# One query tile's rotation earlier, and other places for some of the work beside the matmuls, in a hybrid decoder layer's kernel

## The chip, the cores and the metric

The kernel runs on one core of one Trainium2 chip. The metric is the time of one execution on the device, in microseconds (us). Each kernel is run several times; the median is given with the lowest and the highest. One execution is recorded by the hardware profiler, and all rows come from that one.

## What is computed

A decoder layer in fp32: 512 tokens of 1024 channels. The normalised input is projected once (`h @ w_in`), and the pieces feed two branches, whose outputs are merged by sigmoid gates, projected by `w_out`, added to the input, and followed by a gated convolutional feed-forward layer.

```python
h = rmsnorm(x, norm1_w)
proj = h @ w_in
(mq, mk, mv, mo, mi, mf, nq, kc, vc, ks, vs, kw, vw, ng, gm, gn) = jnp.split(proj, split_pts, axis=-1)
...
hm = mlstm_chunkwise(...)                                  # 4 heads
hm = rmsnorm(hm, m_out_norm_w) * jax.nn.sigmoid(mo)
qn = apply_rope(rmsnorm(nq, q_norm_w), cos, sin)           # 8 heads of 64
...
on = gates[..., 0:1] * o_cmp + gates[..., 1:2] * o_slc + gates[..., 2:3] * o_win
y = jax.nn.sigmoid(gm + merge_gate_b[0]) * (hm @ w_up_m) \
    + jax.nn.sigmoid(gn + merge_gate_b[1]) * (on @ w_up_n)
x = x + y @ w_out
h2 = rmsnorm(x, norm2_w)
a, v = jnp.split(h2 @ ffn_w_up, 2, axis=-1)
a = jax.nn.gelu(causal_dwconv(a, ffn_conv_w, ffn_conv_b), approximate=False)
return x + (a * v) @ ffn_w_down
```

## The kernel before

**Matrix products.** The tokens are worked on in four tiles of 128 (`NT = 4`), the channels in eight groups of 128 (`KD = 8`). An fp32 product is three fp32r products on TensorE (PE): high by high, high by low and low by high, where high is a rounded copy and low is what the rounding left. The class `Weights` brings each weight chunk from memory into one of two raw buffers (`raw`, SP's queue) and `ensure` splits it, half a chunk at a time, into `whl`: four buffers, each with a high and a low half. The high half is a copy by ScalarE (ACT, L88). The low half comes in one of two ways: VectorE (DVE) subtracts (L94), or, for the halves in `on_dma`, ACT makes a negated copy (L91) and GpSimd (POOL) issues a DMA that adds the raw chunk to it (L92). PLAN's `pool...` entries say which: 2 puts a whole group into `on_dma`, and `poolWO` speaks of the first four halves of `w_out` alone.

**Order.** Nothing is scheduled by a tool: every engine works through its own list in the order in which the program wrote it. Two kinds of work are interleaved by hand. One is the layer's latency-bound part (rotation, attention, mLSTM). The other is a stream of projection matmuls, a generator wrapped in the class `Filler`: `fill(ns)` draws three matmuls at a time, each counted as 650 ns, until a balance `bal` is used up. The amounts stand in the table PLAN and are read with `FL(key, default)`. The stream's groups come as A, MV, GM, MO, MQK, GN (the projections of those names), and from the last mLSTM head on UN, the product of `on` with `w_up_n`, then UM, that of `hm` with `w_up_m` (`up_group`). A finished group of matmuls is evacuated by ACT or DVE a few draws later (`after`).

**Banks.** The accumulators lie in eight banks: two of `pa`, two tiles of two banks for `psS`, one `pt`, one `po`. Behind UM these pools are closed, and eight new banks `pf` hold the accumulators of `w_out`, named `wo00` to `wo31` (token tile, column half).

**The places that the change touches, in the order of the run.**

- The rotation of the queries. `rope_q(t)` rotates tile t (L680 to L688 on DVE, a part on POOL) and copies the result to be doubled (`qdup`, L235 on DVE for tiles 0 to 2 and L233 on ACT for tile 3, by PLAN's `p_dupq`). `q_transposes(t)` transposes it on PE into the banks `pt` and `po` (`pq`, L847), and `QS` is made from these by ACT (L849) and DVE (L850). Tile t + 1 is rotated behind the transposes of tile t. The A and MV groups' matmuls run in between (`aV`, `aVs`), and GM's after the last tile.
- The columns of the mLSTM's gates: `rows_b`, a generator stepped from within the attention loop, transposes rows into `uop` (L1083) in the bank `pt`, which the attention's transposes `ptp` use as well.
- The gates' sigmoids: `T["gm"]` (L1253) before the mLSTM's first head, `T["gn"]` (L1277) behind its last, each with ACT's table of functions loaded anew around it (L1255, L1273, L1278).
- The mLSTM's four heads. `mls_s` makes scores `mA` and `mB`, `mls_e` and `mls_x` the exponentials EA and EB, `mls_m` multiplies them (L1129, L1130 on DVE), `mls_b` multiplies by the values (`mo`, L1137 on PE), `mls_c` transposes, gates and splits the result (`hmH`, `hmL`). Between `mls_c(h)` and `mls_m` for head h + 1 the filler gets PLAN's `md{h}`, and before `mls_b` PLAN's `mb{h}`.
- The merge. `evac_un` (L742) and `evac_um` (L1298 to L1307) gate the products and add them. `wo` (L426 to L428) multiplies by `w_out`.
- The loads of x and of the second norm's weights are issued by POOL (L1333, L1335) between the tiles of the first four halves of `w_out`.

```python
    for h in range(4):
        ...
        fill(FL(f"mb{h}", 1000))
        hs, sc, ee = mls_b(h, ee[2], mid)
        ...
        fill(FL(f"mc{h}", 5000))
        mls_c(h, hs)
        if h < 3:
            fill(FL(f"md{h}", 2000))
            mls_m(sc, ee)
```

Of the kernel before, what the change touches and what calls it, by code (L numbers as in the profile page):

```python
# [9 lines left out]
AF = mybir.ActivationFunctionType  # L10
# [8 lines left out]
NT = S // P  # L19
# [78 lines left out]
def bcast(ap, n):  # L98
# [18 lines left out]
    "p_sc21": 0, "p_sc30": 0, "p_sc31": 1, "poolA": 2, "poolC": 0, "poolGM": 2, "poolGN": 2, "poolMO": 2,  # L117
    "poolMQK": 2, "poolMV": 0, "poolUM": 0, "poolUN": 3, "poolWO": 0, "q2_eb": 1, "q2_ex0": 0, "q2_ex1": 0,
# [42 lines left out]
def body(ctx, tc, I, out, dbg=None):  # L161
# [53 lines left out]
    def pt(name):  # L215
        return ps.tile([P, 512], F32, name=name, tag="pt", bufs=1)
# [279 lines left out]
                yield 650  # L496
                tick()

    def up_group(ids, mH, mL, evac, nm, flag):
        for m in range(KD):  # L500
            acc = (psS if m % 2 else pa)(f"{nm}{m}")[:, 0:512]
            W.ensure(ids[m // 2])
            H, L = W.hl[ids[m // 2]]
            w = slice((m % 2) * P, (m % 2) * P + P)
            for k in range(4):
                if k == 2 and m % 2 == 0:
                    W.ensure(ids[m // 2] + 3)
                pe.matmul(acc, H[:, k, w], mH[:, k, :], start=(k == 0), stop=False)
                pe.matmul(acc, H[:, k, w], mL[:, k, :], start=False, stop=False)
                pe.matmul(acc, L[:, k, w], mH[:, k, :], start=False, stop=(k == 3))  # L510
                if k == 3:
                    after(2, lambda m=m, acc=acc: evac(m, acc))
                    if m == KD - 1:
                        after(2, lambda: done.add(flag))
                yield 650
                tick()
# [513 lines left out]
    def rows_b():  # L1030
        ir, fr, t1, t2 = T["rows"]

        act.activation(t1, fr, AF.Abs)
        act.activation(t1, t1, AF.Exp, scale=-1.0)
        dve.tensor_scalar(t2, fr, 0.0, None, op0=ALU.min)
        yield
        act.activation(t1, t1, AF.Ln, bias=1.0)
        yield
        dve.tensor_sub(fr, t2, t1)
        on = onesf[0:4, :]  # L1040
        for c in range(NT):
            q = slice(c * P, (c + 1) * P)
            dve.tensor_tensor_scan(t2[:, q], on, fr[:, q], 0.0, ALU.mult, ALU.add)
        yield
        dve.tensor_sub(ir, ir, t2)
        mc = sm([4, 4], "mc", 1)
        for c in range(NT):
            q = slice(c * P, (c + 1) * P)
            dve.tensor_tensor_scan(fr[:, q], on, ir[:, q], mc[:, c:c + 1] if c else 0.0, ALU.mult, ALU.max)
            if c + 1 < NT:  # L1050
                e = (c + 1) * P - 1
                dve.tensor_add(mc[:, c + 1:c + 2], t2[:, e:e + 1], fr[:, e:e + 1])
        yield

        dve.tensor_add(t1, t2, fr)
        R3 = s4("mrowC", F32R)
        nH, nL = R3[0:4, 0:512], R3[32:36, 0:512]
        pool.tensor_scalar(R3[0:32, 0:512].rearrange("p (a c) -> p a c", a=4),
                           onesf[0:32, :].rearrange("p (o c) -> p o c", o=1).to_broadcast([32, 4, P]), 0.0, None,
                           op0=ALU.mult)  # L1060
        dve.tensor_scalar(fr, fr, -1.0, None, op0=ALU.mult)
        dve.tensor_copy(nH, fr)
        dve.tensor_sub(nL, fr, nH)
        T["nHL"] = R3[0:36, 0:512]
        yield "R4"

        R4 = vst[:, 1024:1792]
        n = 0
        T["urow"] = []
        for k, (i, j) in enumerate(pairs):  # L1070
            if i == j:
                cur = ir[:, j * P:(j + 1) * P]
            else:
                new = R4[0:4, n * P:(n + 1) * P]
                n += 1
                dve.tensor_scalar(new, cur, t2[:, i * P - 1:i * P], None, op0=ALU.add)
                cur = new
            T["urow"].append(cur)

        yield  # L1080
        p = pt("uop")
        for k in range(len(pairs)):
            pe.transpose(p[:, k * 4:k * 4 + 4], T["urow"][k], ident[0:4, 0:4])  # L1083
        for t in range(NT):
            pe.transpose(p[:, 40 + t * 4:44 + t * 4], T["rows"][2][:, t * P:(t + 1) * P], ident[0:4, 0:4])
        dve.tensor_copy(uoc, p[:, 0:40])
        act.activation(emc, p[:, 40:56], AF.Exp, scale=-1.0)
# [119 lines left out]
        rope(qview(t), dup(qd), qrs[:, t * 8:t * 8 + 8], 3, t, 1, 8, f"q{t}")  # L1207
        return qd

    qd = rope_q(0)  # L1210
    fill(FL("z14", 3900))
    for t in range(NT):
        q_transposes(t, qd)
        if t + 1 < NT:
            qd = rope_q(t + 1)
        if t == 1:
            pc0 = cmp_scores(0)
        if t == 2:
            cmp_exp(0, pc0)
        fill(FL(f"z16_{t}", 2600))  # L1220
        if t == 2:
            cmp_scale(0, pc0)
        if t == 3:
            cmp_transposes(0, pc0)
# [21 lines left out]
    for z in range(2):  # L1246
        mz = T["mo"][:, 2 * z:2 * z + 2, :]
        act.activation(mz, mz, AF.Sigmoid)
        fill(FL("z25", 1300))
    for i in range(2):  # L1250
        for z in range(2):
            g = T["gm"][i][:, 2 * z:2 * z + 2, :]
            act.activation(g, g, AF.Sigmoid)  # L1253
            fill(FL("z26", 1300))
    act.preload_act_table_set(LNEXP)  # L1255
    T["hmH"] = v4(page("hmH", F32R))
    sc = mls_s(0)
# [4 lines left out]
    for h in range(4):  # L1262
        if h < 3:
            mid = (lambda: mls_s(h + 1), lambda n: mls_e(h + 1, n), mls_x)
        else:
            mid = (lambda: None, lambda n: None, lambda n: None)
        fill(FL(f"mb{h}", 1000))
        hs, sc, ee = mls_b(h, ee[2], mid)
        if h == 3:
            fill.until(done, "GN")  # L1270
            fill = Filler(up_group(F_UN, T["onH"], T["onL"], evac_un, "un", "UN"), flush)
            W.ensure(F_UN[3])
            act.preload_act_table_set("sigmoid_and_others")  # L1273
            for i in range(2):
                for z in range(2):
                    g = T["gn"][i][:, 2 * z:2 * z + 2, :]
                    act.activation(g, g, AF.Sigmoid)  # L1277
            act.preload_act_table_set(LNEXP)  # L1278
        fill(FL(f"mc{h}", 5000))
        mls_c(h, hs)  # L1280
        if h < 3:
            fill(FL(f"md{h}", 2000))
            mls_m(sc, ee)
# [22 lines left out]
    def y_low(m):  # L1306
        dve.tensor_sub(act4(yL, m), T["gm"][m // 4][:, m % 4, :], act4(yH, m))  # L1307

    fill = Filler(up_group(F_UM, T["hmH"], T["hmL"], evac_um, "um", "UM"), flush)
    fill(1e9)  # L1310
    ps_cm.close()

# [336 lines left out]
```

## Time and profile before

| | |
|---|---|
| median of 3 runs | 793.24 us (791.92 to 793.84) |
| the profiled execution, its own time | 793.33 us |
| its span in the trace | 791.6 us |
| TensorE's mean granted clock | 0.998 of full speed |
| PE busy | 775.5 us, 98% of the span |
| DVE busy | 471.5 us, 60% |
| ACT busy | 371.1 us, 47% |
| POOL busy | 208.5 us, 26% |
| moved by DMA | 126.93 MB, 160 GB/s on average |

The span runs from the first to the last instruction of the core; the execution's own time has the start and the end around it, 1.7 us here. An engine's busy time is the time in which it worked on an instruction. PE's share is an upper bound of its use, since the ends of its pipelined matmuls are modelled. Times of rows are counted from the span's start: the query tiles' transposes lie at 97 to 117 us, the attention at 120 to 280, the mLSTM's heads at 290 to 349, UN and UM up to 393, `w_out` up to 425, and the feed-forward layer fills the rest.

### The profile page before, as it was taken

Reading aid. Unit: us, or ns where it says so; the run is one execution under the profiler, and the core shown is the slowest. Engines: PE = TensorE matmul, PEld = TensorE weight load, DVE = VectorE, ACT = ScalarE, POOL = GpSimd, SP = SyncE. Lnnn points to the kernel's source line nnn. Section 1 sums busy time; section 2 is a strip of 40 time slices with the busy share of each in tenths; the row PEclk is TensorE's granted clock in tenths of the full one; section 3 lists DMA queues with packets and bytes.
Section 4 is the critical chain, followed back from the end, with each engine's and each line's share of the span. In section 5 each row is a group of like instructions: output and inputs, shape, how many; then the busy total and the mean of one; then the engine's idle time right before and its main releaser. Section 6 shows DMA issues by size and latency. Waiting matters only on the chain.

```text
span 791.6 us, 10531 instructions
## 1 busy us (share of the span) xinstructions
PE 775.5 (98%) x4037; PEld 641.7 (81%) x4037; DVE 471.5 (60%) x827; ACT 371.1 (47%) x627; POOL 208.5 (26%) x217
## 2 busy tenths in 40 slices
PE   7999989999999999989999999999999999999997
PEld 5797878877888887878788998888888888888886
DVE  4576785676565654556755455455454554565865
ACT  6254536745565586464333243334334333455441
POOL 4420122120111113120000017854555443200700
PEclk9999999999999999999999999999999999999999
DMA  7884167655547476563263248665555434585472
GB/s 229 286 220 142 21 150 122 117 107 107 108 89 125 82 105 128 112 212 121 94 209 111 107 152 293 245 228 199 212 189 184 179 140 160 199 279 188 145 236 84
DMA packets 93314, 126.93 MB, mean 160 GB/s; under 512 B 6447, under 2 KB 72143, under 8 KB 91856
## 3 DMA queue, kind: packets, MB, share of 16 engines
q1 hardware_dynamic: 63054, 91.64, 34.8%
q0 software_dynamic: 30208, 34.61, 21.0%
q8 instruction: 32, 0.52, 0.3%
q14 instruction: 18, 0.15, 0.1%
q10 hardware_dynamic: 2, 0.00, 0.0%
HBM read 94.79 MB, written 15.73 MB: 140 GB/s over the span
## 4 chain that ended last, share of the span: by engine, by line
PE 84%; DVE 8%; ACT 4%; issue 1%; DMA 1%; SPq 0%; DVEq 0%; ACTq 0%
PE ff L1366 10%; PE ff L1365 10%; PE ff L1364 10%; PE P L427 4%; PE P L428 4%; PE P L426 4%; PE on L947 2%; PE ptp L936 2%; PE wo L426 2%; PE wo L428 2%; PE wo L427 2%; PE gm L488 1%; PE gm L490 1%; PE gm L489 1%; PE sp L906 1%
## 5 line engine op out<-in xcount | busy, mean ns | idle before, releaser
L94 DVE TENSOR_TENSOR whl<-raw,whl 128x1024 fp32r<-128x1024 f32 (+1 forms) x112 | 141.4, 1275 | 139.1 <-ACT whl L88 139.1
L88 ACT ACTIVATE whl<-raw 128x1024 fp32r<-128x1024 f32 (+2 forms) x144 | 144.8, 1012 | 121.2 <-PE ff L1366 57.1
L1364 PE MATMUL ff<-h2H,whl 128*128 128x512 f32 (+1 forms) x384 | 142.8, 372 | 0.0
L1365 PE MATMUL ff<-h2L,whl 128*128 128x512 f32 (+1 forms) x384 | 142.6, 371 | 0.0
L1366 PE MATMUL ff<-h2H,whl 128*128 128x512 f32 (+1 forms) x384 | 142.6, 371 | 0.0
L92 POOL DMA_DIRECT2D whl<-raw x30 | 43.6, 1454 | 183.7 <-ACT whl L91 175.6
L1365 PEld LDWEIGHTS ff<-h2L,whl 128*128 128x128 f32 x384 | 72.3, 188 | 12.6
L1364 PEld LDWEIGHTS ff<-h2H,whl 128*128 128x128 f32 x384 | 72.3, 188 | 12.5
L1366 PEld LDWEIGHTS ff<-h2H,whl 128*128 128x128 f32 x384 | 72.3, 188 | 12.4
L921 ACT ACTIVATE P<-sp,nmx 128x128 f32<-128x128 f32 (+3 forms) x64 | 33.1, 524 | 36.7 <-DVE nmx L912 36.5
L1416 ACT ACTIVATE ct<-ct 128x512 f32<-128x512 f32 x22 | 13.9, 634 | 54.1 <-DVE ct L1414 54.1
L912 DVE TENSOR_REDUCE nmx<-sp 128x2 f32<-128x256 f32 (+3 forms) x32 | 26.2, 818 | 17.9 <-PE sp L909 17.8
L426 PE MATMUL P<-whl,g 128*128 128x512 f32 x88 | 34.2, 389 | 0.0
L427 PE MATMUL P<-whl,g 128*128 128x512 f32 x88 | 34.2, 389 | 0.0
L428 PE MATMUL P<-whl,g 128*128 128x512 f32 x88 | 34.2, 389 | 0.0
L1414 DVE SCALAR_TENSOR_TENSOR ct<-ff,vcol,ct 128x511 f32<-128x511 f32 (+1 forms) x44 | 32.8, 744 | 2.2 <-ACT ct L1412 1.4
L91 ACT ACTIVATE whl<-raw 128x1024 fp32r<-128x1024 f32 x30 | 31.5, 1050 | 0.0
L1422 ACT ACTIVATE g<-ct 128x512 fp32r<-128x512 f32 x22 | 13.9, 634 | 37.0 <-DVE ct L1426 21.9
L235 DVE COPY P<-ptp 128x256 f32<-128x256 f32 (+1 forms) x32 | 17.7, 554 | 19.3 <-PE ptp L936 19.2
L1423 DVE TENSOR_TENSOR g<-ct,g 128x512 fp32r<-128x512 f32 x22 | 15.4, 699 | 22.0 <-ACT g L1422 22.0
L1355 POOL DMA_DIRECT2D x1d<-x x4 | 2.1, 536 | 95.1 <-DVE x L1354 95.1
L488 PE MATMUL gm<-hTH,whl 128*128 128x512 f32 x64 | 26.6, 416 | 0.0
(400 smaller groups left out, 1811.8 us busy)
## 6 DMA issues: line engine op xcount, KB each, us to landing
raw<-in_ffn_w_up_dram SPq DMA_DIRECT2D x22, 1024.0 KB, 5.1
raw<-in_w_in_dram SPq DMA_DIRECT2D x16, 1024.0 KB, 4.9
whl<-raw POOLq DMA_DIRECT2D x30, 512.0 KB, 5.7
st<-in_ffn_w_down_dram SPq DMA_DIRECT2D x11, 1024.0 KB, 7.0
td<-st POOLq DMA_DIRECT2D x11, 1024.0 KB, 4.1
raw<-td SPq DMA_DIRECT2D x22, 512.0 KB, 5.2
raw<-in_ffn_w_down_dram SPq DMA_DIRECT2D x11, 512.0 KB, 4.6
raw<-in_w_out_dram SPq DMA_DIRECT2D x4, 1024.0 KB, 4.9
```

The source lines that it names most:

```text
L88: nc.scalar.activation(h, src, AF.Copy)
L92: nc.gpsimd.dma_start(l, src, accum_op=ALU.add)
L94: (nc.gpsimd if n in self.on_pool else nc.vector).tensor_sub(l, src, h)
L426: pe.matmul(o, aH, bH, start=start, stop=False)
L427: pe.matmul(o, aH, bL, start=False, stop=False)
L428: pe.matmul(o, aL, bH, start=False, stop=stop)
L488: pe.matmul(acc, H[:, k, :], hh, start=(k == 0), stop=False)
L921: act.activation(Pv[:, y], sv[:, y], AF.Exp, bias=nmx[:, y:y + 1], accum_out=den[:, y:y + 1])
L1364: pe.matmul(acc[:, a:b], H[:, k, :], hh, start=(k == 0), stop=False)
L1365: pe.matmul(acc[:, a:b], H[:, k, :], hl, start=False, stop=False)
L1366: pe.matmul(acc[:, a:b], L[:, k, :], hh, start=False, stop=(k == KD - 1))
L1414: dve.scalar_tensor_tensor(t[:, k:], a[:, :S - k], col("ffn_conv_w", (2 - k) * NF + m), t[:, k:], op0=ALU.mult, op1=ALU.add)
```

## The change

Six things move; no arithmetic is left out or added.

- `rope_q` runs one tile ahead: tiles 0 and 1 before the loop, tile t + 2 behind the transposes of tile t.
- `rows_b` draws three matmuls more ahead of `uop`, and takes their 650 ns off the balance again.
- The four sigmoids of `gm` go from ahead of the first head to behind `mls_c(3)`, one before every 1300 ns of filler, and the table load behind `gn`'s sigmoids goes behind them.
- `md2` becomes 0: the multiplications of the last head follow `mls_c(2)` at once, and the filler that stood between them comes after.
- `up_group` gets a list `wide` of the groups that go to `psS` banks: it was the odd ones; now it is 1, 3, 6, 7 for UN and 1, 6, 7 for UM.
- `poolWO` becomes 2: the low halves of `w_out`'s first four weight halves come from L91 and the DMA of L92.

```diff
-    "mc0": 4675, "mc1": 5000, "mc2": 5000, "mc3": 11500, "md0": 3950, "md1": 3625, "md2": 15275, "ms0": 6300,
+    "mc0": 4675, "mc1": 5000, "mc2": 5000, "mc3": 11500, "md0": 3950, "md1": 3625, "md2": 0, "ms0": 6300,
...
-    "poolMQK": 2, "poolMV": 0, "poolUM": 0, "poolUN": 3, "poolWO": 0, "q2_eb": 1, "q2_ex0": 0, "q2_ex1": 0,
+    "poolMQK": 2, "poolMV": 0, "poolUM": 0, "poolUN": 3, "poolWO": 2, "q2_eb": 1, "q2_ex0": 0, "q2_ex1": 0,
...
-    def up_group(ids, mH, mL, evac, nm, flag):
+    def up_group(ids, mH, mL, evac, nm, flag, wide):
         for m in range(KD):
-            acc = (psS if m % 2 else pa)(f"{nm}{m}")[:, 0:512]
+            acc = (psS if m in wide else pa)(f"{nm}{m}")[:, 0:512]
...
         yield
+        fill(650)
+        fill.bal -= 650
         p = pt("uop")
...
-    qd = rope_q(0)
+    qds = [rope_q(0), rope_q(1)]
     fill(FL("z14", 3900))
     for t in range(NT):
-        q_transposes(t, qd)
-        if t + 1 < NT:
-            qd = rope_q(t + 1)
+        q_transposes(t, qds[t])
+        if t + 2 < NT:
+            qds.append(rope_q(t + 2))
...
-    for i in range(2):
-        for z in range(2):
-            g = T["gm"][i][:, 2 * z:2 * z + 2, :]
-            act.activation(g, g, AF.Sigmoid)
-            fill(FL("z26", 1300))
     act.preload_act_table_set(LNEXP)
...
-            fill = Filler(up_group(F_UN, T["onH"], T["onL"], evac_un, "un", "UN"), flush)
+            fill = Filler(up_group(F_UN, T["onH"], T["onL"], evac_un, "un", "UN", (1, 3, 6, 7)), flush)
...
-            act.preload_act_table_set(LNEXP)
         fill(FL(f"mc{h}", 5000))
         mls_c(h, hs)
+        if h == 3:
+            for i in range(2):
+                for z in range(2):
+                    fill(1300)
+                    g = T["gm"][i][:, 2 * z:2 * z + 2, :]
+                    act.activation(g, g, AF.Sigmoid)
+            act.preload_act_table_set(LNEXP)
...
-    fill = Filler(up_group(F_UM, T["hmH"], T["hmL"], evac_um, "um", "UM"), flush)
+    fill = Filler(up_group(F_UM, T["hmH"], T["hmL"], evac_um, "um", "UM", (1, 6, 7)), flush)
```

How this moves instructions is shown at three places, where a queue's order decides. Rows are an engine's instructions in its own order: line, operation, out<-in, shape. Lines of the changed kernel are two or three higher there from `uop` on.

ACT from the QS of query tile 1 to that of tile 2, before:

```order
L849 ACTIVATE QS_859<-pq_1070 128x512
L849 ACTIVATE QS_859<-pq_1077 128x512
L233 ACTIVATE vst<-sc_1092 128x256
L88 ACTIVATE whl_1104<-raw_910 128x1024
L91 ACTIVATE whl_1104<-raw_910 128x1024
L849 ACTIVATE QS_860<-pq_1123 128x512
L849 ACTIVATE QS_860<-pq_1130 128x512
L233 ACTIVATE qdup_1137<-qdup_1137 128x8x64
```

and with the change:

```order
L849 ACTIVATE QS_859<-pq_1078 128x512
L849 ACTIVATE QS_859<-pq_1085 128x512
L233 ACTIVATE qdup_1092<-qdup_1092 128x8x64
L233 ACTIVATE vst<-sc_1100 128x256
L88 ACTIVATE whl_1112<-raw_910 128x1024
L91 ACTIVATE whl_1112<-raw_910 128x1024
L849 ACTIVATE QS_860<-pq_1131 128x512
L849 ACTIVATE QS_860<-pq_1138 128x512
```

The copy of the rotated tile 3 (`qdup`) stood behind the QS of tile 2 (`QS_860`); it now stands ahead of the copy of the scores (`vst`), of the weight half (`whl`, L88 and L91) and of that QS.

DVE from the end of head 2 to the multiplications of the last head (`EA`, `EB` with `mA`, `mB`), before:

```order
L1167 SCALAR_TENSOR_TENSOR hs_3257<-mhT_3327,vcol,mo 128x512
L1169 TENSOR_TENSOR hmL<-hs_3257,hmH 128x512
L94 TENSOR_TENSOR whl_3337<-raw_3182,whl_3337 128x1024
L1129 SCALAR_TENSOR_TENSOR EA_3263<-mA_3236,EA_3263 128x896
L1130 SCALAR_TENSOR_TENSOR EB_3264<-mB_3237,EB_3264 128x384
L1143 TENSOR_TENSOR mad<-mad,emc 128x4
```

and with the change:

```order
L1169 SCALAR_TENSOR_TENSOR hs_3253<-mhT_3323,vcol,mo 128x512
L1171 TENSOR_TENSOR hmL<-hs_3253,hmH 128x512
L1131 SCALAR_TENSOR_TENSOR EA_3259<-mA_3232,EA_3259 128x896
L1132 SCALAR_TENSOR_TENSOR EB_3260<-mB_3233,EB_3260 128x384
L94 TENSOR_TENSOR whl_3335<-raw_3178,whl_3335 128x1024
L1145 TENSOR_TENSOR mad<-mad,emc 128x4
```

The subtraction for a weight half (L94) stood ahead of the multiplications and now stands behind them.

POOL from the last heads' masks on (`EA_`, `EB_`) to the writes of the new x (`x1d`), before:

```order
L1124 AFFINE_SELECT EA_3263<-EA_3263 128x128 x2
L1124 AFFINE_SELECT EB_3264<-EB_3264 128x128 x2
L92 DMA whl_3297<-raw_3036 128x4x256
L1333 DMA x_0_3537<-in_x_dram 128x1024 x2
L1335 DMA nw_3540<-in_norm_w_dram 128x1024
L1333 DMA x_1_3538<-in_x_dram 128x1024 x2
L1355 DMA x1d<-x_0_3537 128x1024 x2
```

and with the change:

```order
L1126 AFFINE_SELECT EA_3259<-EA_3259 128x128 x2
L1126 AFFINE_SELECT EB_3260<-EB_3260 128x128 x2
L92 DMA whl_3293<-raw_3032 128x4x256
L92 DMA whl_3590<-raw_3511 128x1024
L92 DMA whl_3628<-raw_3511 128x1024
L92 DMA whl_3668<-raw_3588 128x1024
L92 DMA whl_3724<-raw_3588 128x1024
L1336 DMA x_0_3537<-in_x_dram 128x1024 x2
L1338 DMA nw_3540<-in_norm_w_dram 128x1024
L1336 DMA x_1_3538<-in_x_dram 128x1024 x2
L1358 DMA x1d<-x_0_3537 128x1024 x2
```

Four DMAs for the low halves of `w_out` (`whl_3590` to `whl_3724`) are new, and the loads of x and of the norm's weights (`nw`) stand behind them.

## Rows read from the trace of the kernel before

**Rows 1.** who PE waited for: us in total, times, longest us

```profile
PE mo L1137 <- DVE EA L1129: 2.1, 1, 2.1
...
PE pq L847 <- DVE qdup L235: 1.8, 3, 1.1
...
PE wo L426 <- DVE gm L1298: 1.0, 1, 1.0
...
PE gn L488 <- ACT gn L719: 0.6, 1, 0.6
PE pq L847 <- ACT qdup L233: 0.6, 1, 0.6
PE uop L1083 <- DVE P L235: 0.5, 1, 0.5
```

**Rows 2.** timeline of PE in a dense run: start us, us, engine, line, operation, out<-in

```profile
206.18 0.40 PE L489 MATMUL mo<-hTL,whl 128*128 128x512 f32 x1
206.41 0.39 PE L490 MATMUL mo<-hTH,whl 128*128 128x512 f32 x1
```

**Rows 3.** timeline of DVE at the rotation: [idle before <-releaser] at the end

```profile
93.05 0.69 DVE L680 TENSOR_TENSOR qraw<-qraw,rrs 128x512 f32<-128x512 f32 x1
...
96.18 0.52 DVE L235 COPY qdup<-qdup 128x512 f32<-128x512 f32 x1
96.61 1.21 DVE L94 TENSOR_TENSOR whl<-raw,whl 128x1024 fp32r<-128x1024 f32 x1
98.14 1.30 DVE L850 TENSOR_TENSOR QS<-pq,QS 64x512 fp32r<-64x512 f32 x2 [0.32 <-ACT QS L849]
...
116.36 0.69 DVE L235 COPY mv<-aV 128x512 f32<-128x512 f32 x1
```

**Rows 4.** timeline of ACT at the rotation

```profile
106.54 1.05 ACT L91 ACTIVATE whl<-raw 128x1024 fp32r<-128x1024 f32 x1
...
115.57 0.63 ACT L233 ACTIVATE qdup<-qdup 128x512 f32<-128x512 f32 x1 [3.99 <-DVE qdup L688]
```

**Rows 5.** timeline of PE at the transposes of the query tiles

```profile
96.84 1.07 PE L847 MATMUL pq<-ident,qdup 128*128 128x128 f32 x8 [0.32 <-DVE qdup L235]
...
116.25 1.09 PE L847 MATMUL pq<-ident,qdup 128*128 128x128 f32 x8 [0.57 <-ACT qdup L233]
```

**Rows 6.** DMA issues: KB each, median us from issue to landing

```profile
whl<-raw POOLq DMA_DIRECT2D x30, 512.0 KB, 5.7
...
x<-in_x_dram POOLq DMA_DIRECT2D x4, 512.0 KB, 9.4
```

**Rows 7.** timeline of ACT ahead of the mLSTM's first head

```profile
292.05 3.89 ACT L1253 ACTIVATE gm<-gm 128x1024 f32<-128x1024 f32 x4
```

**Rows 8.** timeline of ACT behind the last head

```profile
353.22 1.28 ACT L1273 ACT_TABLE_LOAD   x1
354.51 3.91 ACT L1277 ACTIVATE gn<-gn 128x1024 f32<-128x1024 f32 x4
...
365.80 1.07 ACT L88 ACTIVATE whl<-raw 128x1024 fp32r<-128x1024 f32 x1 [0.27 <-PE un L510]
```

**Rows 9.** timeline of PE, first matmul of um

```profile
371.04 0.39 PE L508 MATMUL um<-hmH,whl 128*128 128x512 f32 x1
```

**Rows 10.** timeline of DVE ahead of the last head's mo

```profile
342.44 1.23 DVE L94 TENSOR_TENSOR whl<-raw,whl 128x1024 fp32r<-128x1024 f32 x1 [0.25 <-ACT whl L88]
343.58 1.08 DVE L1129 SCALAR_TENSOR_TENSOR EA<-mA,EA 128x896 f32<-128x896 f32 x1
```

**Rows 11.** windows: us, busy per engine, granted clock (PEclk), DMA share, GB/s

```profile
344.00:348.00 4.00, 3.19 (x15) 3.22 (x16) 1.13 (x2) 0.17 (x1) 0.68 (x2) 0.61 1.06 257
392.00:394.00 2.00, 1.00 (x6) 0.53 (x4) 1.97 (x3) 0.00 (x0) 0.00 (x0) 1.00 0.00 0
```

**Rows 12.** timeline of ACT, high halves of w_out's first four weight halves

```profile
378.67 1.05 ACT L88 ACTIVATE whl<-raw 128x1024 fp32r<-128x1024 f32 x1
...
397.05 2.94 ACT L88 ACTIVATE whl<-raw 128x1024 fp32r<-128x1024 f32 x3
```

## The prediction

> **What bounds the kernel now.** Read the table of busy times first: TensorE (PE) is busy for 98% of the span, the next engine for 60%. Work of PE is neither added nor taken away, so what can be won is what PE waits. The view of who waited for whom gives that directly [rows 1]: mo for EA (2.1 us), pq for qdup (1.8 in three waits, and 0.6), wo for gm (1.0), gn for gn (0.6), uop for P (0.5). The parts of the change answer to these one by one.
>
> Two things on pricing such a wait. Idle time is counted from the listed end of the matmul before: a listed matmul lasts 0.39 us, but the next of a dense run starts 0.23 later [rows 2]. So each wait is, from start to start, about 0.16 longer than its entry. And behind the merge no wait of PE is long enough for an entry in rows 1, so I count what is won earlier as won at the end.
>
> **The change part by part**, on the clock of the profiled run.
>
> *Rotation one tile ahead.* DVE takes 3.6 us for one tile's rotation with its copy (93.05 to 96.6), 3.1 without the copy, 1.2 for the low part of a weight half and 1.3 for both QS of a tile [rows 3]. Before, each rotation began behind QS of the tile before it, and PE came for the tile too early. The change starts tile 1 before the loop. I walk DVE by these durations: tile 1 from 96.6 to 100.2, the half to 101.3, QS of tile 0 to 102.6; tile 2 to 106.2, QS of tile 1 to 107.5; tile 3 to 110.6. Tiles 1 and 2 are there before PE.
>
> But tile 3's copy is ACT's, and in ACT's queue (first pair of order fences) it now stands ahead of the scores' copy, both passes of a weight half and QS of tile 2, which used to be ahead of it. The second of those passes began at 106.54 and takes 1.05 like the first; tile 3's copy takes 0.63 [rows 4]. So ACT now stands until the rotation is through, near 110.6, and comes to QS of tile 2 at 110.6 + 0.6 + 2.1, near 113.3; DVE's part of it ends near 115.2. Tile 3's transposes write over tile 2's banks. They began at 116.25 [rows 5]; without the waits before them PE is there near 114.2, and waits some 0.5. Next GM's first matmul needs the bank that DVE's copy of mv frees. That copy ended at 117.05 [rows 3], and behind the late QS it ends near 116.85. What is won at the first three waits is lost at these two: **0.2 us**. Ends: 0, if ACT's queue is that much slower; 2.1, if none of it reaches PE (rows 1: 1.8 + 0.6, less the first tile's 0.3 [rows 5], which stays). Of these I take the walked value. The late weight half's accumulating DMA lands 5.7 after its issue [rows 6], near 119, and GM's second group begins 24 matmuls (5.4 us) after 116.9: nothing.
>
> *Columns' transposes.* Three mo matmuls (0.69 by rows 2) that stood behind the scores now run while uop waits for P's copy, and the filler's balance is put back, so none is added. The wait is 0.5 [rows 1], 0.66 from start to start: **0.65**, ends 0 and 0.69.
>
> *Gates' sigmoids.* Four sigmoids of gm (3.89 us from 292.05 [rows 7]) stand ahead of ACT's table load, head 0's exponentials and the copy of gn for which PE waits 0.6 [rows 1]. Without them that copy moves up by nearly 3 us (the exponentials then wait for DVE). The whole wait goes: **0.8**, ends 0 and 0.8.
>
> They come back behind the last head, with the table load after them. The weight half that ACT began at 365.80 [rows 8] then begins near 369.3, behind the last head's copy, another half, 3.9 us of sigmoids and 1.3 of load. DVE's low part of it (1.2) and the evacuation of un6 (0.7) queue behind it and end near 372.2. um's second group needs un6's bank 12 matmuls, or 2.7 us, after 371.04 [rows 9]: 373.8. I cost it at nothing; the cover is 1.5 us, and a microsecond beyond it is a microsecond lost. In rows 8 a load of 1.28 starts at 353.22 and the next ACT instruction at 354.51, at once. The Trainium skill (ScalarE: Activation LUTs, What ACT_TABLE_LOAD costs) adds a drain of about 1.38 us to the load; by that, un6's evacuation would end near 373.6 and the cover be 0.2, the sum the same. The trace does not agree; rival 3 gets a little of its chance from it.
>
> *Last head's multiplications.* Before, DVE was free at 342.2, waited 0.25 for ACT, made the low part of a half (342.44, 1.23) and only then EA (343.58, 1.08) [rows 10]; PE, out of filler, waited 2.1, or 2.2 from start to start. Now EA stands ahead of the half (second pair of fences): 342.2 to 343.2, and PE goes on near 343.3 instead of 344.8. **1.5** are won, a wait of 0.7 stays; ends 0 and 2.2.
>
> Behind this wait the granted clock is 0.61 from 344 to 348 us [rows 11], a mix of the two levels, 2.4 and 1.2 GHz: 4 x (1 - 0.61) = 1.56 us of full-speed work lost. From 392 to 394 PE stands idle for 1.0 us and the granted clock stays 1.00 [rows 11]. A wait of 0.7 is nearer to that one, so I take the clock's **1.5** as won; ends 0 and 1.6.
>
> *Banks of the merge, and w_out's low halves.* With um's groups on other banks, wo's first matmul takes a bank whose reader is long done; the groups that meet um6's and um7's banks come 9 and 15 matmuls later (2.0 and 3.4 us). The wait of 1.0 goes [rows 1]: **1.15**, ends 0 and 1.2. For each of four low halves ACT takes a second pass (1.05) and POOL an accumulating DMA (5.7 to its landing [rows 6]) in place of DVE's 1.2. The first of these halves begins on ACT at 378.67 [rows 12], so it lands near 386.5; wo needs it when um's 96 matmuls are through, 371.04 + 21.8 = 392.8. The fourth begins at 397.05 [rows 12], lands near 404.9 and is needed 72 matmuls later, at 409.1. Cover 6.3, falling to 4.2: nothing on the path. The loads of x and of the norm's weights are now behind these four DMAs in POOL's queue (third pair of fences). They go out from about 400 and take 9.4 [rows 6]; x is first added when w_out's first tile is whole, 96 + 24 matmuls or 27 us after 392.8. Nothing.
>
> *Sum:* 0.2 + 0.65 + 0.8 + 1.5 + 1.5 + 1.15 = 5.8. The profiled run took 793.33, 0.09 above the median shown (793.24): **787.5 us**.
>
> **The rivals.**
>
> 1. *The waits go whole.* ACT's queue at the rotation doesn't reach PE (2.1 instead of 0.2), and EA comes 0.7 earlier still. For it: both hang on places in queues that I walked by hand. Against: ACT's order holds QS. 5.8 + 1.9 + 0.7 = 8.4: 784.9.
>
> 2. *The clock falls all the same.* PE meets 0.7 of idle and then the same short multiplications. Against: the second stretch of rows 11. 1.5 less: 789.0.
>
> 3. *um waits for un6's bank.* The late sigmoids and their load use up the cover of 1.5 and as much again (1.4). For it: ACT's queue there holds five things whose starts I moved. 788.9.
>
> 4. *w_out's low halves come late*, the slower side. They go through POOL's queue one after another, and the fourth stalls PE once it lands over 5.7 + 4.2 = 9.9 us after its ACT passes; each microsecond more is one lost. The nearest slow row, the loads of x with 9.4 on the same queue [rows 6], just doesn't do it. At 20 us, 10.1 are lost: 787.5 + 10.1 = 797.6; to end above the time before by over 0.3% it takes 18. The Trainium skill (DMA: Bandwidth & Descriptors, SWDGE vs HWDGE vs iDMA) says that GpSimd writes such a DMA's descriptors into SBUF, from which DVE shuts it out in its 2-port mode; no run here shows which of DVE's merge work is in that mode. The 30 DMAs of this kind landed in a median of 5.7 with DVE at work beside them, so this adds little to the chance.
>
> 5. *Nothing comes through.* PE's waits go, and the same time turns up as new waits in the feed-forward part, where weights come in behind PE all the time: about 793.2.
>
> **How the numbers follow.** 0.3% (2.4 us) is about what a measurement of this kernel can tell from no change, so faster means under 790.9. Chances: the forecast 0.52, rival 1 0.12, rival 2 0.15, rival 3 0.08, rival 4 0.05, rival 5 0.08. Faster: the first four, 0.87; same: rival 5, 0.08; slower: rival 4, 0.05. The range leaves out rivals 4 and 5 (0.13): from rival 1's 784.9, rounded down to 784.8, to rivals 2 and 3 together, 787.5 + 1.5 + 1.4 = 790.4.
>
> **What would show it.** Right: no entry for gn, uop and wo in the view of waits, and one of about 0.6 for mo; a granted clock of 1.00 in the four microseconds behind it; between 107 and 116 us an ACT that stands for DVE's rotation, PE's waits there moved to tile 3's pq and to gm; the accumulating DMAs x34. Wrong: a wait of wo for whl or for a DMA, of um for gn, a half clock behind a wait of 0.7, or new entries behind 420 us.

## The result, and the profile after

| | before | the change |
|---|---|---|
| median, same runs | 793.36 us (791.92 to 793.84, 4 runs) | 786.93 us (786.64 to 787.16, 4 runs) |
| ratio | | 0.9923, 95% interval 0.9911 to 0.9936 |
| profiled execution, its own time | 793.33 us | 786.64 us |

The change is faster by 0.8%: 6.4 us between the medians, where 5.8 had been forecast. The page of the changed kernel, its span, the engines' busy times and DVE's and POOL's groups for the weights' low halves:

```profile
span 784.8 us, 10544 instructions
...
PE 773.2 (99%) x4037; PEld 640.5 (82%) x4037; DVE 466.5 (59%) x823; ACT 374.5 (48%) x631; POOL 211.3 (27%) x221
...
L94 DVE TENSOR_TENSOR whl<-raw,whl 128x1024 fp32r<-128x1024 f32 (+1 forms) x108 | 136.5, 1276 | 148.7 <-ACT whl L88 148.7
...
L92 POOL DMA_DIRECT2D whl<-raw x34 | 47.1, 1384 | 234.9 <-ACT whl L91 183.9
```

PE has the same 4037 matmuls. Four low halves have gone from DVE's subtraction to POOL's DMA (x34 instead of x30). Who PE waited for in the changed kernel (us in total, times, longest us), to be laid beside [rows 1]:

```profile
PE gm L488 <- DVE mv L235: 1.0, 1, 1.0
PE pq L847 <- DVE QS L850: 0.9, 1, 0.9
...
PE mo L1139 <- DVE EA L1131: 0.6, 1, 0.6
...
PE pq L847 <- DVE qdup L235: 0.2, 1, 0.2
```

The entries of wo, gn and uop are gone, mo waits 0.6 instead of 2.1, and pq for qdup has only the first tile's wait left. Two entries are new, both at the rotation.

**Where the time went.** The same matmul can be looked up in both traces. How much earlier PE starts it in the changed kernel, in us, read at both ends of each place (0.2 of it is there from the kernel's first matmul groups on, ahead of every change):

| place | PE earlier, ahead of it | behind it | won there | forecast |
|---|---|---|---|---|
| rotation (from pq of tile 0 to gm's first matmul) | 0.23 | 0.41 | 0.2 | 0.2 |
| uop, with the three matmuls moved ahead of it | 0.37 | 0.95 | 0.6 | 0.65 |
| gn before the first head | 0.96 | 2.03 | 1.1 | 0.8 |
| last head, the wait | 2.03 | 3.51 | 1.5 | 1.5 |
| last head, the clock | 3.51 | 5.16 | 1.65 | 1.5 |
| wo | 5.15 | 6.39 | 1.25 | 1.15 |
| the feed-forward part | 6.39 | 6.38 | 0 | 0 |

The two profiled executions differ by 6.7 (793.33 and 786.64); the 0.3 that the table leaves lie outside PE's matmuls. PE's rows before, at gm's first matmul and at the last head:

```profile
117.10 0.50 PE L488 MATMUL gm<-hTH,whl 128*128 128x512 f32 x1
344.81 2.47 PE L1137 MATMUL mo<-mv,EA 128*128 128x129 f32 x10 [2.06 <-DVE EA L1129]
348.68 0.47 PE L508 MATMUL un<-onH,whl 128*128 128x512 f32 x1
```

and of the changed kernel, for the last head:

```profile
341.30 1.35 PE L1139 MATMUL mo<-mv,EA 128*128 128x129 f32 x10 [0.57 <-DVE EA L1131]
343.52 0.48 PE L508 MATMUL un<-onH,whl 128*128 128x512 f32 x1
```

From mo to un's first matmul PE takes 3.87 before and 2.22 with the change; the difference is the clock's 1.65.

**The rotation.** In the changed kernel PE reaches the last matmul of the projections between the tiles 2.19 earlier and gm's first one only 0.41 earlier. Its timeline there (start us, us, engine, line, operation, out<-in, and in brackets the idle time before with what ended it):

```profile
102.24 1.03 PE L847 MATMUL pq<-ident,qdup 128*128 128x128 f32 x8
...
107.69 1.03 PE L847 MATMUL pq<-ident,qdup 128*128 128x128 f32 x8
...
114.45 1.26 PE L847 MATMUL pq<-ident,qdup 128*128 128x128 f32 x8 [0.95 <-DVE QS L850]
116.69 0.50 PE L488 MATMUL gm<-hTH,whl 128*128 128x512 f32 x1 [0.98 <-DVE mv L235]
```

and ACT's:

```profile
110.39 0.63 ACT L233 ACTIVATE qdup<-qdup 128x512 f32<-128x512 f32 x1 [6.42 <-DVE qdup L688]
110.92 0.36 ACT L233 ACTIVATE vst<-sc 128x256 f32<-128x256 f32 x1
111.19 1.05 ACT L88 ACTIVATE whl<-raw 128x1024 fp32r<-128x1024 f32 x1
112.14 1.04 ACT L91 ACTIVATE whl<-raw 128x1024 fp32r<-128x1024 f32 x1
113.08 1.07 ACT L849 ACTIVATE QS<-pq 128x512 fp32r<-128x512 f32 x2
```

and DVE's:

```profile
109.66 0.69 DVE L688 TENSOR_TENSOR qdup<-rtq 128x512 f32<-128x512 f32 x1
...
113.70 1.30 DVE L850 TENSOR_TENSOR QS<-pq,QS 64x512 fp32r<-64x512 f32 x2 [1.96 <-ACT QS L849]
...
115.94 0.69 DVE L235 COPY mv<-aV 128x512 f32<-128x512 f32 x1
```

ACT stands for 6.42 us until DVE has rotated tile 3; QS of tile 2, whose transposes were through at 108.7, comes only at 113.08. DVE in turn stands 1.96 for ACT, and its copy of mv starts at 115.94, 0.4 earlier than in [rows 3]. gm's first matmul starts 0.05 behind that copy's end before (116.36 + 0.69 and 117.10) and 0.06 behind it after (115.94 + 0.69 and 116.69).

**The last head.** DVE of the changed kernel makes EA straight behind hmL, and the low half after it:

```profile
340.07 1.08 DVE L1131 SCALAR_TENSOR_TENSOR EA<-mA,EA 128x896 f32<-128x896 f32 x1
...
341.54 1.21 DVE L94 TENSOR_TENSOR whl<-raw,whl 128x1024 fp32r<-128x1024 f32 x1
```

These answer to [rows 10]. In the windows of the changed kernel (us, busy per engine, granted clock as the last figure but two) the clock stays, where [rows 11] had 0.61:

```profile
340.00:342.00 2.00, 1.43 (x10) 0.99 (x9) 2.00 (x4) 1.06 (x2) 0.00 (x0) 1.00 0.88 142
342.00:344.00 2.00, 2.00 (x18) 1.96 (x18) 0.75 (x1) 0.34 (x2) 0.00 (x0) 1.00 0.82 133
344.00:346.00 2.00, 2.00 (x11) 1.63 (x10) 0.34 (x2) 1.42 (x7) 0.00 (x0) 1.00 0.30 30
```

**The covers.** ACT behind the last head, with the moved sigmoids and table load:

```profile
358.85 3.88 ACT L1282 ACTIVATE gm<-gm 128x1024 f32<-128x1024 f32 x4
362.75 1.28 ACT L1283 ACT_TABLE_LOAD   x1
364.04 1.06 ACT L88 ACTIVATE whl<-raw 128x1024 fp32r<-128x1024 f32 x1
```

DVE's evacuations of un6 and un7 in one row, and PE's first matmul of um's second group, which needs un6's bank:

```profile
366.28 1.28 DVE L742 TENSOR_TENSOR gn<-gn,un 128x512 f32<-128x512 f32 x2
```

```profile
368.61 0.39 PE L508 MATMUL um<-hmH,whl 128*128 128x512 f32 x1
```

Each evacuation takes 0.68, so un6's ends near 366.96, 1.65 ahead of need; the forecast had 1.5 of cover. The instruction behind the load starts at once, 362.75 + 1.28 = 364.03. The Trainium skill (ScalarE: Activation LUTs, What ACT_TABLE_LOAD costs) has a drain of about 1.38 us there; estimated with that figure, un6's bank would have been free only 0.3 ahead of need (1.65 less 1.38). No trace of this case shows such a drain.

POOL's DMAs for w_out's low halves, the first and the last of four, and the loads behind them:

```profile
375.81 0.88 POOL L92 DMA_DIRECT2D whl<-raw  x1 [35.87 <-DVE gm L1302]
...
392.12 0.86 POOL L92 DMA_DIRECT2D whl<-raw  x1 [4.58 <-ACT whl L91]
392.66 1.43 POOL L1336 DMA_DIRECT2D x<-in_x_dram  x2
```

They land in a median of 5.7 us like the others, and nothing waits for them.

**The wait of wo before.** On DVE a low half of w_out, itself held by ACT, stood ahead of the evacuation of um6, which is the one that wo's first matmul waited for [rows 1]:

```profile
392.00 1.23 DVE L94 TENSOR_TENSOR whl<-raw,whl 128x1024 fp32r<-128x1024 f32 x1 [1.05 <-ACT whl L88]
393.14 0.68 DVE L1298 TENSOR_TENSOR gm<-gm,um 128x512 f32<-128x512 f32 x1
```

The evacuation ended at 393.82, and wo's first matmul started at 393.96, 1.39 behind um's last. In the changed kernel it starts 0.23 behind it (387.65 and 387.42).

### The profile page after: what moved, and what is told of

Read it like the earlier page. It is cut to its first block, busy times and chain, and to the rows that moved or that the text cites. A ratio compares the mean times of both kernels' runs of the same rounds, so it can differ in the third digit from the quotient of the medians.

```text
span 784.8 us, 10544 instructions
## 1 busy us (share of the span) xinstructions
PE 773.2 (99%) x4037; PEld 640.5 (82%) x4037; DVE 466.5 (59%) x823; ACT 374.5 (48%) x631; POOL 211.3 (27%) x221
## 4 chain that ended last, share of the span: by engine, by line
PE 90%; DVE 7%; ACT 2%; issue 1%; POOL 0%; DVEq 0%; POOLq 0%
PE ff L1368 10%; PE ff L1367 10%; PE ff L1369 10%; PE P L427 4%; PE P L428 4%; PE P L426 4%; PE on L947 2%; PE ptp L936 2%; PE wo L426 2%; PE wo L427 2%; PE wo L428 2%; PE gn L488 2%; PE gn L490 2%; PE gn L489 2%; PE gm L488 1%; PE gm L490 1%
## 5 line engine op out<-in xcount | busy, mean ns | idle before, releaser
L94 DVE TENSOR_TENSOR whl<-raw,whl 128x1024 fp32r<-128x1024 f32 (+1 forms) x108 | 136.5, 1276 | 148.7 <-ACT whl L88 148.7
L88 ACT ACTIVATE whl<-raw 128x1024 fp32r<-128x1024 f32 (+2 forms) x144 | 144.8, 1012 | 126.4 <-PE ff L1369 57.2
L92 POOL DMA_DIRECT2D whl<-raw x34 | 47.1, 1384 | 234.9 <-ACT whl L91 183.9
L1367 PEld LDWEIGHTS ff<-h2H,whl 128*128 128x128 f32 x384 | 72.3, 188 | 12.6
L91 ACT ACTIVATE whl<-raw 128x1024 fp32r<-128x1024 f32 x34 | 35.7, 1049 | 0.0
L427 PE MATMUL P<-whl,sb 128*128 128x512 f32 x66 | 25.9, 393 | 0.2
```

The source lines that it names most:

```text
L88: nc.scalar.activation(h, src, AF.Copy)
L91: nc.scalar.activation(l, src, AF.Copy, scale=-1.0)
L92: nc.gpsimd.dma_start(l, src, accum_op=ALU.add)
L94: (nc.gpsimd if n in self.on_pool else nc.vector).tensor_sub(l, src, h)
L427: pe.matmul(o, aH, bL, start=False, stop=False)
L1367: pe.matmul(acc[:, a:b], H[:, k, :], hh, start=(k == 0), stop=False)
```

## The experiments

Twelve kernels were run, the change itself among them, each against the kernel before. The start varies from one execution to the next: in the traces aB waits between 0.8 and 2.1 us for hTH, and by 80 us PE stands up to 2.4 later or 0.6 earlier than in the change's trace. Where less than a microsecond matters, I therefore read PE's place in the trace at the same matmul, against the trace of the change, and take the difference from one side of a place to the other.

A part of what moves the start can be seen. In six of the fourteen traces (the copy on DVE, the rotation back, the wait as before, the gates back, uop back, both) 6 to 12 of the first matmuls of aB last 0.63 us and start 0.43 apart, instead of 0.39 and 0.23. PE of the rotation back, and its window:

```profile
14.21 0.63 PE L427 MATMUL aB<-whl,hTH 128*128 128x512 f32 x1
14.63 0.63 PE L428 MATMUL aB<-whl,hTL 128*128 128x512 f32 x1
```

```profile
14.00:16.00 2.00, 2.00 (x6) 1.52 (x6) 1.69 (x5) 2.00 (x3) 0.00 (x0) 1.00 0.54 205
```

The matmuls of gm have the same times where the granted clock reads 0.50 (next run). At the start it reads 1.00 in five of the six traces and falls in one, that of the gates back (0.50 from 14 to 16 us). So an execution's mean granted clock, which is all that is on record of those that were not traced, neither tells where the clock fell nor counts every slow stretch.

**The change once more**, as the measure for three others.

> The change itself, once more, as the measure for the other three of this call: about 786.9, with the granted clock at 0.999 to 1.00 in every execution, since the wait of 0.6 that is left before the last head's mo does not make it fall.

787.28 us (787.07 to 788.23, 5 runs), ratio 0.9933 (0.992 to 0.9945). The clock was not what was expected: 0.997 to 0.999 as the mean over the executions. The trace has a fall, but not behind the last head. It comes behind the two new waits at the rotation, in the windows

```profile
114.00:116.00 2.00, 1.26 (x8) 0.83 (x8) 1.90 (x5) 0.21 (x2) 1.03 (x1) 1.00 0.19 24
116.00:118.00 2.00, 1.31 (x3) 1.12 (x4) 1.86 (x6) 2.00 (x3) 0.00 (x0) 0.68 1.46 188
118.00:120.00 2.00, 2.00 (x6) 1.52 (x6) 0.87 (x3) 1.71 (x4) 1.44 (x1) 0.50 0.50 59
120.00:122.00 2.00, 2.00 (x12) 1.59 (x10) 1.25 (x2) 0.60 (x1) 0.10 (x1) 0.96 0.86 108
```

A gm matmul starts 0.43 us behind the one before it there instead of 0.23, and PE loses 1.6 us over eight of them. The change's first trace has 1.00 in the same windows.

**The copy of tile 3 on DVE.**

```diff
-    ... "p_dupq3": 0,
+    ... "p_dupq3": 1,
```

> The change, but the copy of the rotated tile 3 is made by DVE instead of ACT. Theory (ACT's queue gave back what the earlier rotation won): ACT makes the weight half near 104 to 106 and QS of tile 2 as soon as its transposes are there, so PE's waits for QS (0.95) and for mv (0.98) both go; gm's first matmul starts near 114.4 instead of 116.69 and the time is about 784.7, 2.2 below the change. Rival (DVE itself is full there, with its own copy on top): one of the two waits stays and the time is within 0.7 of the change's 786.9.

785.02 us (783.98 to 785.94, 4 runs), ratio 0.9905 (0.989 to 0.992). Neither wait is left; PE's timeline of that kernel:

```profile
114.34 1.03 PE L847 MATMUL pq<-ident,qdup 128*128 128x128 f32 x8
115.28 0.50 PE L488 MATMUL gm<-hTH,whl 128*128 128x512 f32 x1
```

This execution had started 1.0 later than the change's; at gm's first matmul it is 1.41 ahead: 2.4 won. So it was ACT's queue, held by one copy, that gave back what the earlier rotation wins; DVE has room for the copy.

**The rotation back.** The old loop, the rest of the change kept.

> The change without the rotation one tile ahead. Theory: the rotation was worth 0.2 us net, so about 787.1, with the three waits of pq back and those for QS and mv gone. Rival (the earlier rotation brought its whole 2.0): about 788.9.

786.8 us (786.24 to 788.91, 4 runs), ratio 0.9933 (0.9915 to 0.9951). PE is 2.19 later than in the change at 80 us, by the start, and 2.37 later at gm: the rotation in the change is worth 0.2 us, as forecast. The times alone could not tell that from nothing. The old waits are back (qdup 1.8 in three and 0.6).

**md2 back.**

```diff
-    ... "md2": 0,
+    ... "md2": 15275,
```

> The change with md2 at 15275 again, so that the weight half's subtraction stands ahead of the last head's multiplications. Theory: the wait of 2.06 comes back (1.5 more) and the granted clock falls behind it (1.65 more): about 790.0, PE behind mo 3.1 later than in the change. Rival (the clock fell for another reason, that the change has also removed): 1.5 more, about 788.4, with a granted clock of 1.00 behind the wait.

790.25 us (787.91 to 791.41, 10 runs), ratio 0.9967 (0.9955 to 0.9979): by the median the theory's 790.0. But the traced execution, the fastest of the ten, has the wait of 2.1 and a clock of 1.00 behind it:

```profile
PE mo L1139 <- DVE EA L1131: 2.1, 1, 2.1
```

```profile
342.00:344.00 2.00, 1.25 (x11) 1.28 (x12) 1.06 (x2) 0.17 (x1) 0.00 (x0) 1.00 0.82 130
344.00:346.00 2.00, 2.00 (x16) 1.82 (x16) 0.34 (x2) 0.24 (x2) 0.00 (x0) 1.00 0.32 23
```

PE is 1.5 later and no more. Its mean clock was 0.999. Of the ten, seven have a mean clock of 0.998 or less, at 790.6 on average, and three are above, at 788.5; where it fell in the seven is not on record. Behind a wait of 2.06, then, the clock fell in the trace of the kernel before and did not fall in this one.

**The wait as before, without the old order.**

```diff
+            if h == 2:
+                for _ in range(8):
+                    dve.tensor_copy(onesf, ident)
             mls_m(sc, ee)
```

> The change, with eight copies of 128x128 on DVE ahead of the last head's multiplications, into a tile that nothing reads any more: the wait is made as long as before (about 2.1) without the order of before. Theory (the length of PE's wait decides on the clock): the granted clock falls to about half behind the wait for some 3.5 us, and the time is 2.7 to 3.4 above the change, about 790. Rival (something else in the old order made the clock fall): only the wait's 1.5, about 788.4, clock 1.00.

790.7 us (788.95 to 792.1, 9 runs), ratio 0.9979 (0.9967 to 0.999). The copies made the wait 2.5 rather than 2.1. The clock falls in the trace:

```profile
342.00:344.00 2.00, 0.68 (x3) 0.71 (x4) 2.00 (x4) 0.00 (x0) 0.00 (x0) 0.83 0.80 126
344.00:346.00 2.00, 2.00 (x11) 2.00 (x11) 0.77 (x1) 0.17 (x1) 0.00 (x0) 0.50 0.40 69
346.00:348.00 2.00, 2.00 (x14) 1.87 (x13) 0.29 (x2) 0.17 (x1) 0.00 (x0) 0.81 1.03 402
```

PE loses 2.0 by the longer wait and 1.65 by the clock. Eight of nine executions have a mean clock of 0.998 or less. In the traced one the clock fell without the old order, so that order isn't needed for it.

**A wait in between.** The same with four copies.

> The change, with four copies of 128x128 on DVE ahead of the last head's multiplications: by the eight of the earlier run, the wait for EA grows from 0.6 to about 1.5. Theory (each wait costs its length, and a long one sometimes a fall of the clock on top): the trace shows mo 1.0 later than in the change, and a fall of the clock behind it in some executions only, fewer than with 2.5; the median is 788.0 to 788.8. Rival (the clock falls behind any wait over one microsecond): it falls in nearly all, about 789.6.

787.81 us (787.32 to 789.03, 5 runs), ratio 0.9946 (0.9934 to 0.9959). A wait of 1.5, mo 0.9 later in the trace, a clock of 1.00 behind it, and four of five executions at 1.00 on average, with times of 787.3 to 787.9. The rival falls.

**The old banks**, with the low halves left with POOL: `(1, 3, 5, 7)` for both groups.

> The change with the old banks of UN and UM (odd groups in psS), and w_out's low halves left with ACT and POOL. Theory (the wait of wo came from DVE's queue, where a low half stood ahead of um6's evacuation; either part of the change removes it): no wait of wo, within 0.2 of the change. Rival (the bank is what matters, wo's first accumulator meets um6's bank too early whatever DVE does): a wait of wo for gm of 0.5 to 1.0, so 787.5 to 788.1.

787.75 us (786.4 to 788.26, 4 runs), ratio 0.9932 (0.9919 to 0.9946). No wait of wo; PE is within 0.1 of the change from 80 us to the end. The new banks are worth nothing once DVE has no low half ahead of um6's evacuation.

**The low halves back with DVE**, the new banks kept: `"poolWO": 0`.

> The change with w_out's first four low halves made by DVE again, and the new banks kept. Theory (either part removes the wait): um6's evacuation is late again behind a low half, but the group that needs its bank comes 2.0 us after the end of um, so no wait of wo: within 0.2 of the change. Rival: wo or um waits 0.3 to 1.0 for DVE, so 787.2 to 788.1.

788.6 us (787.43 to 788.74, 4 runs), ratio 0.9941 (0.9926 to 0.9956). wo doesn't wait, so either part removes that wait, as the theory has it; that it comes back with both undone was not run. But another wait has come, which no theory had. In the view of waits of that kernel:

```profile
PE un L508 <- DVE gn L742: 0.5, 1, 0.5
```

and on its ACT, for a half of w_up_m's first chunk:

```profile
356.30 1.06 ACT L88 ACTIVATE whl<-raw 128x1024 fp32r<-128x1024 f32 x1 [2.12 <-DMA raw<-in_w_up_m_dram]
```

With what the next matmuls lose behind that wait, PE falls 0.8 further behind the change there (from 0.92 to 1.72). The chunk's load was issued at 346.1. The loads of x and the norm's weights (2.5 MB) had gone out from 340.3 on, since nothing stood ahead of them in POOL's queue. The trace also has a fall of the clock at the rotation, so by time alone nothing could be told here.

**The same, with those loads behind ACT's work.**

```diff
-        pool.dma_start(x1[i], x[i * P:(i + 1) * P, :])
+        act.dma_start(x1[i], x[i * P:(i + 1) * P, :])
...
-            pool.dma_start(nw2, bcast(I["norm2_w"], D))
+            act.dma_start(nw2, bcast(I["norm2_w"], D))
```

> The change with w_out's low halves made by DVE (as in the run that put them back), but with the loads of x and of the norm's weights issued by ACT, behind its work for w_out's first halves. Theory (the wait of un for gn of 0.5 came from a load of w_up_m's chunk that shared the DMA engines with these loads, issued from 340 us on): no wait of un, PE in the trace within 0.2 of the change. Rival (un waited for DVE's own order with the low halves): the wait of 0.5 is there again.

788.74 us (786.86 to 789.24, 4 runs), ratio 0.9952 (0.9939 to 0.9966). The wait of un is gone; the load of w_up_m takes a median of 5.0 us to land instead of 7.3. This execution had the fall of the clock at the rotation (0.65 and 0.50 from 116 to 120 us), and behind it PE keeps its distance from the change to the end. So the loads' place was the cause.

**The gates' sigmoids back** ahead of the first head, the table load left where the change has it.

> The change with the four sigmoids of gm ahead of the first head again. Theory: the wait of gn for ACT's copy comes back, 0.8 with what the next matmuls lose behind it up to 1.1: gn's matmul there and all behind it 0.8 to 1.1 later in the trace. Rival (the late sigmoids cost something behind the last head that this gives back): less than 0.5 at the end.

788.55 us (788.48 to 790.35, 5 runs), ratio 0.996 (0.9947 to 0.9973). The wait of gn for ACT's copy is 0.6 again, and PE goes from 0.92 later ahead of it to 1.97 behind it: 1.05. Less than 0.1 is given back behind the last head. The trace has a granted clock of 0.94 in its first 30 us and 1.00 at the rotation and the last head.

**uop back**, without the three matmuls ahead of it.

> The change without the three matmuls ahead of uop. Theory: the wait of 0.5 comes back and PE is 0.65 later behind it in the trace. Rival (the matmuls only moved the wait to the next transposes): no difference behind the next scores.

788.43 us (787.08 to 789.32, 4 runs), ratio 0.9951 (0.9938 to 0.9965). The wait of 0.5 is back, and PE goes from 2.29 to 2.86 later: 0.6.

**Both: the copy on DVE, and UN's first matmuls ahead of the last head's mo.**

```diff
+        if h == 3:
+            fill.until(done, "GN")
+            fill = Filler(up_group(F_UN, T["onH"], T["onL"], evac_un, "un", "UN", (1, 3, 6, 7)), flush)
+            fill(650)
         hs, sc, ee = mls_b(h, ee[2], mid)
         if h == 3:
-            fill.until(done, "GN")
-            fill = Filler(up_group(F_UN, T["onH"], T["onL"], evac_un, "un", "UN", (1, 3, 6, 7)), flush)
```

> The change with two more edits: the copy of tile 3's rotation on DVE, and UN's first three matmuls ahead of the last head's mo. Theory: the waits for QS, mv and EA are all gone, so PE ends 2.4 + 0.6 = 3.0 earlier than in the change: about 783.9. Rival (the matmuls that fill the wait only move it, because un0's weight half or its bank comes later): about 784.5, the gain of the copy alone.

784.01 us (783.76 to 784.26, 4 runs), ratio 0.9888 (0.9874 to 0.9901), against 787.28 for the change on the same chip. It beats both kernels. PE goes straight from un's matmuls to mo:

```profile
338.98 0.39 PE L510 MATMUL un<-onH,whl 128*128 128x512 f32 x1
339.26 1.35 PE L1139 MATMUL mo<-mv,EA 128*128 128x129 f32 x10
```

From the rotation on PE is 2.4 earlier than in the change, and 0.7 more behind the last head (from 0.43 later at 80 us to 2.72 earlier). Behind the start no wait over 0.3 is left in the view of waits.

## Why the prediction was right

The time lay 0.6 below the forecast, and each step's place and sign were found again. Three sizes came out larger, and each passed the upper end that the prediction gave for its step: the gates by 0.3, the clock by 0.15, wo by 0.1. In the profiled executions the gain is 6.7, 0.9 over the forecast's 5.8: 0.4 come from the steps, and 0.5, at the start and outside PE's matmuls, belong to no step and are chance as far as is known.

- *The rotation, 0.2.* Right, and by the mechanism forecast: ACT's queue, shown by taking one copy out of it (2.4 us won). The two waits that take the old ones' place were sized too small at the first: 0.95 for QS instead of 0.5, because PE came at 113.5 and not at 114.2. I had taken the three old waits off by their listed 2.1 and forgotten the 0.16 each that I had priced them with, and the earlier start. The sum didn't suffer, since gm is tied to the copy of mv, which I had at 116.85 and which ended at 116.63.
- *uop, 0.65.* Right: 0.6, and 0.6 again when it was put back.
- *The gates, 0.8.* Place and mechanism right, the term mis-sized: 1.05 to 1.1. The wait itself is 0.8. The rest is lost behind it: in the kernel before, the matmuls of gn and of the first mo that follow the wait start 0.1, 0.08 and 0.08 later, each against the one ahead, than in the changed kernel.
- *The last head's wait, 1.5.* Right to 0.02.
- *The clock's 1.5.* Right for the traced executions (1.65), but the step behind it was too simple, and that the size came out was in part luck. I had the wait's length decide. At 2.06 the clock fell in the trace of before and not in that of md2 back, so the term is there only against an execution in which the old kernel's clock fell. How often that is, no run shows. Over 37 more executions of the kernel before, 19 have a mean clock of 0.998 or less; they take 793.0 on average and the other 18 792.2, but where the clock fell in them is not known. The mean of the 37 is 792.6 and that of the nine executions of the change 787.3, which makes 5.3 rather than 6.4. The forecast's 5.8 lies between.
- *The merge, 1.15.* Right in size: 1.25, of which 0.1 is lost behind the wait. Of its two parts I gave the whole to the banks. The runs show that either removes the wait, and that holding back x's loads, which I had down at nothing, is worth something: with the low halves back on DVE these loads meet the load of w_up_m and cost 0.8 at un, 0.5 of it listed as a wait. The kernel before sent these loads early too, but ACT came to w_up_m's first half 12.6 us after the issue of its load (347.16 to 359.73), and in the run with the low halves back it was free for it after 8.1 (346.07 to 354.18).
- *The rivals.* The first (the waits go whole) describes the kernel with the copy on DVE and the filled wait, not the change. The second (the clock falls all the same) didn't happen at the last head; it happened at the rotation, in three traces of the kernels that keep the change's two waits there. I had looked for it in the wrong place. Third, fourth and fifth: nothing of them in the trace.

What stays open: in which executions the clock falls. It is not the kernel alone: of the two traces of the change one has a fall at the rotation and one has none.

## What to carry to other kernels

A value made earlier can be worth next to nothing (0.2 of 2.4 us here) if the engine that copies it works in order and other results stand behind that copy: walk the copying engine's queue too, and give the copy to the engine that makes the value. Fill a wait of the matmul engine with other matmuls rather than shorten it: what is left of it costs its length, and a wait of 2 us cost a drop of the clock of nearly the same size again in some executions. When a transfer is held back by something that you remove, ask which transfer it will now meet.

## What the runs showed of the hardware

- The granted clock fell to its half level (1.2 of 2.4 GHz) behind a wait of PE of 2.06 us in one trace and not in another, behind one of 2.54 us in the one traced, behind one of 1.5 us not in the one traced, and behind two waits of 0.95 and 0.98, with eight transposes between them, in three of ten traces. Each of these five falls cost 1.4 to 1.65 us.
- At the start, behind a wait of 0.8 to 2.1 us, matmuls ran 0.43 us apart instead of 0.23 in six of fourteen traces, and the granted clock read 1.00 over them in five of the six. The other eight had waits of 0.8 to 1.7 there.
- A wait costs more than its idle time: behind the wait of gn the next matmuls started 0.26 late in sum at an unchanged clock, behind that of wo 0.08.
- The start, which is the same program in all kernels, differed by up to 2.7 us between traces at 30 us, from the loads to the first matmul groups.
